# A decoder layer on one core: smaller DMA scratch, probability buffers of two heads, and other places for the feed-forward's tiles

## The chip, the cores and the metric

The kernel is one program on one core of a Trainium2 chip. The metric is the device time of one execution in microseconds (us), lower is better. A core has five engines that run side by side, each through its own list of instructions in a fixed order: TensorE (PE, with weight loads shown as PEld), VectorE (DVE), ScalarE (ACT), GpSimd (POOL) and SyncE (SP, which here only starts DMAs). They meet through semaphores. SBUF is the on-chip memory with 128 partitions, PSUM holds matmul results.

## The reference, in short

One decoder layer over 1024 tokens of width 1024, in float32:

```
h = x + RMSNorm_post(Mixer(RMSNorm_pre(x)))
out = h + RMSNorm_post(SwiGLU(RMSNorm_pre(h)))

Mixer: proj = hn @ w_in; split into q, k/v of three branches, gates, u, v
  8 heads (2 groups of keys and values), each with three attention branches, biased by relative position:
    compressed blocks | selected blocks of 64 (top 16 of 16: all causal ones) | sliding window of 512
    o = gate0 * o_c + gate1 * o_s + gate2 * o_w        (a softmax in each branch)
  8 gMLP groups: gelu(u) * (causal w_s @ layer_norm(gelu(v)) + b_s)
  concat -> @ w_out
SwiGLU: (silu(h2 @ w_gate) * (h2 @ w_up)) @ w_down,  width 2816
```

## The kernel before

A float32 product is made of three matmuls: each operand is split into a high and a low part (`split`, line 167 on ACT for the high part, line 173 on DVE or POOL for the low one), and `mm3` (lines 183 to 185) adds hi x hi, hi x lo and lo x hi.

**Order of the work.** The program is written with a framework that puts every instruction in the order of its engine beforehand. `tc.high_priority(...)` moves a block ahead in that order (`HP`, `HP2` the logits, `HO` and `HF` the output projection and the norm behind it, `HQ` the loads of q, `HS` the normalization, `HV` the products with v); the framework also sets the semaphore waits, for data and for buffers that have to come free. Order and waits are fixed when the program is built.

1. *Projections and gMLP*, until about 248 us. The transposed inputs `xTh0`, `xTl0`, `xTh1`, `xTl1` are read by the last projections (`v_proj`).
2. *Attention*, from 248 to about 593 us: query tiles 7, 6, ..., 0 of 128 tokens; in a tile two groups with two head pairs each, 32 pairs in all (pairs 0 to 3 are tile 7, 16 to 19 tile 3, 20 to 23 tile 2, 28 to 31 tile 0). For a head PE computes logits into PSUM (banks `ps_a`, two of them), DVE adds the bias and takes the extremes while writing them into a buffer `L` (lines 655 and 659), ACT applies exp in place (698). For the pair POOL normalizes in place (709), PE transposes (722), ACT and DVE split (`ph`, `pl`), PE multiplies with `vt` and `vch` (729), and the result is split into `mixh` and `mixl`. `load_q` loads `qr` for the pair after next through SP and lets POOL split it into `qt`. In the second pair of the next tile `output_proj` is placed (its inputs `gmh` are loaded by POOL's queue, `xt` by SP's), in the last pair `pre_ffn`, which writes the normed rows `h2s` to `h2_scr` in DRAM.
3. *Feed-forward*. The tokens are halves 0 and 1, the inner dimension is halves too. `raw1` (half 1, name `b_r1t` in the trace) is loaded from `h2_scr` in four DMAs (779), `plain_raw` (the first weights) in four (790). Eight weight operands (four in `plain_op`, four in the ring `op`) and `b12`, `b22` are split from them, and `plain_pass(1)` makes the first 256 hidden columns for half 1 with 96 matmuls; `plain_pass(0)` does the same for half 0 with `raw0`, `b11`, `b21`. All other hidden columns are made by Strassen-Winograd pairs (`prep_pair`, `run_pair`), 20 units of seven products, with `t1` to `t4` made from `raw0` and `raw1`. They end at about 1034 us.
4. *Down projection* until 1249 us, with the hidden values reloaded from DRAM (`hidr`).

**Memory.** SBUF of a partition is given out from two ends: a left stack above the scratch of dynamic DMAs (16,384 bytes before), and a right stack down from the top. A pool that is opened later on the place of a closed one makes its first writers wait for the last users of each tile that lay there. The left stack in attention is, from below: constants, the rings `whi` and `wlo`, `pt`, `mix`, `late` (`gpost`, `xt`, `h1`, `gmh`, `h2s`), six `L` buffers of 6,912 bytes, `o` (`otmp`, `os`), `q` (`qr`, `qt`). On the right lie `kt0`, `kt1`, `vch`, `vt` and the bias tables `B`, `C`, `MW`. The six buffers `L0` to `L5` (L0 the lowest) are given to the heads in turn from the top, L5, L4, ..., L0, then L5 again. The seven feed-forward tiles of 16 KB each (`r1t4`, `b22`, `b12t3`, `t1`, `t2`, `b11`, `b21`) are opened on the right after attention; `plain_raw` uses the place of `b11`, `plain_op` that of `t1`, `b12` that of `b12t3`. Worked out from the sizes, before: `r1t4` lies where `kt0`, `kt1` and `vch` lay, `b22` on `vt`, `b12t3` on `vt` and the bias tables, `t1` on L5, `o` and `q`, `b11` on L0 to L2, `b21` on `late` and L0.

## Time and profile before

| what | value |
|---|---|
| time, median of 3 runs | 1255.89 us (1254.95 to 1257.32) |
| profiled execution | 1254.52 us, span from first to last instruction 1252.8 us |
| mean granted clock of TensorE | 0.987 of full speed |
| PE busy | 1212.1 us (97%), 6074 instructions |
| PEld busy | 1011.5 us (81%) |
| DVE busy | 918.8 us (73%) |
| ACT busy | 566.0 us (45%) |
| POOL busy | 400.8 us (32%) |

The span is that of the profiled execution, which took 1.4 us less than the median of the runs. Busy shares are means over stages with different limits. A clock of 0.50 is 1.2 GHz, 1.00 is 2.4 GHz. In a timeline a row gives start, duration, engine, line of the code, operation, written and read tiles, and in brackets the idle time of the engine before it with what ended it; xN means N instructions in a row that were put together.

### The profile page before, as it was taken

What the parts mean: (1) busy time and instruction counts of PE and PEld (TensorE: products, weight loads), DVE (VectorE), ACT (ScalarE), POOL (GpSimd) and SP (SyncE); (2) the same over time, 40 slices, a digit from 0 to 9 for tenths busy, and PEclk for the clock granted to TensorE, in tenths of its full rate; (3) what the DMA queues carried; (4) which work ended last, traced back from release to release, by engine and by line L of the source; (5) the groups of instructions that cost most, each with busy time, mean ns of one, the idle gap of its engine ahead of it and who ended that gap; (6) DMA issues with size and microseconds to landing.
All of it is one profiled execution on the core that took longest, in us unless ns stands there. A gap on an engine that the chain in (4) does not pass through costs nothing. (4 is left out here: it accounts for less than half of the span.)

```text
span 1252.8 us, 18246 instructions
## 1 busy us (share of the span) xinstructions
PE 1212.1 (97%) x6074; PEld 1011.5 (81%) x6074; DVE 918.8 (73%) x2064; ACT 566.0 (45%) x1260; POOL 400.8 (32%) x467
## 2 busy tenths in 40 slices
PE   6999999989999999999999999999999999999996
PEld 5888878968888888887777888888888888888885
DVE  5646247479788899876689877877787647588996
ACT  3423022157677778875644332333332324544541
POOL 2415112178445455642151222201221201132433
PEclk9999999979999999999899999999999999999999
DMA  7313452142221221213714333223233189333335
GB/s 251 88 66 86 134 187 78 57 133 60 66 58 43 65 64 62 75 56 106 272 40 140 107 118 127 93 88 109 90 126 126 55 284 363 113 110 85 101 120 191
DMA packets 106229, 143.86 MB, mean 115 GB/s; under 512 B 8120, under 2 KB 64792, under 8 KB 106136
## 3 DMA queue, kind: packets, MB, share of 16 engines
q1 hardware_dynamic: 99408, 132.90, 32.7%
q10 hardware_dynamic: 4424, 5.61, 1.3%
q0 software_dynamic: 2304, 4.20, 1.2%
q8 instruction: 48, 0.79, 0.3%
q14 instruction: 45, 0.37, 0.1%
HBM read 103.60 MB, written 40.71 MB: 115 GB/s over the span
## 5 line engine op out<-in xcount | busy, mean ns | idle before, releaser
L937 DVE TENSOR_TENSOR cc<-fb,cc 128x512 f32<-128x512 f32 x140 | 94.3, 686 | 59.4 <-PE fb L185 58.5
L709 POOL TENSOR_SCALAR L<-L,wts 128x64 f32<-128x64 f32 (+8 forms) x192 | 107.6, 584 | 83.7 <-DVE wts L704 50.2
L698 ACT ACTIVATE L<-L,mm 128x64 f32<-128x64 f32 (+8 forms) x192 | 116.2, 607 | 30.6 <-DVE mm L655 29.9
L826 POOL TENSOR_TENSOR cc<-sil 128x512 f32<-128x512 f32 x22 | 34.9, 1587 | 289.0 <-issue 227.2
L173 DVE TENSOR_TENSOR pl<-ps_t,ph 128x512 fp32r<-128x512 f32 (+2 forms) x168 | 102.8, 618 | 13.5 <-ACT ph L167 12.7
L167 ACT CAST ph<-ps_t 128x512 fp32r<-128x512 f32 (+2 forms) x168 | 87.4, 532 | 43.5 <-PE ps_t L722 37.5
L167 ACT CAST op<-s 128x512 fp32r<-128x512 f32 x80 | 49.4, 621 | 122.2 <-PE fb L185 109.3
L184 PE MATMUL fb<-wdo,hido 128*128 128x512 f32 x264 | 102.7, 389 | 0.0
L183 PE MATMUL fb<-wdo,hido 128*128 128x512 f32 x264 | 101.9, 389 | 0.0
L185 PE MATMUL fb<-wdo,hido 128*128 128x512 f32 x264 | 100.4, 389 | 0.0
L184 PE MATMUL fb<-b_b,op 128*128 128x512 f32 x256 | 99.6, 389 | 0.0
L185 PE MATMUL fb<-b_b,op 128*128 128x512 f32 x256 | 99.4, 389 | 0.0
L183 PE MATMUL fb<-b_b,op 128*128 128x512 f32 x256 | 99.3, 389 | 0.0
L722 PE MATMUL ps_t<-ident,L 128*128 128x128 f32 (+1 forms) x592 | 94.9, 278 | 1.1 <-DVE mm L655 0.5
L650 PE MATMUL ps_a<-kt,qt 128*128 128x448 f32 (+4 forms) x208 | 78.0, 379 | 7.1 <-DVE L L659 4.3
L173 DVE TENSOR_TENSOR hido<-hidr,hido 128x512 fp32r<-128x512 f32 x77 | 60.6, 799 | 27.2 <-ACT hido L167 27.0
L1016 POOL TENSOR_TENSOR tt<-wdr 128x512 f32<-128x512 f32 x22 | 36.0, 1642 | 134.7 <-DVE wdo L173 80.0
L722 PEld LDWEIGHTS ps_t<-ident,L 128*128 128x128 f32 (+1 forms) x592 | 69.4, 139 | 9.9 <-POOL L L709 1.4
L167 ACT CAST hido<-hidr 128x512 fp32r<-128x512 f32 x77 | 47.3, 619 | 66.3 <-PE fb L185 23.2
L167 ACT CAST op<-wraw 128x512 fp32r<-128x512 f32 x60 | 37.0, 622 | 87.3 <-PE fb L185 71.3
L173 DVE TENSOR_TENSOR op<-s,op 128x512 fp32r<-128x512 f32 x80 | 63.3, 796 | 16.3 <-ACT op L167 15.6
L729 PE MATMUL ps_p<-ph,vt 128*128 128x256 f32 x264 | 73.2, 295 | 0.2 <-ACT ph L167 0.2
(351 smaller groups left out, 3480.0 us busy)
## 6 DMA issues: line engine op xcount, KB each, us to landing
wraw<-in_w_gate_up_dram SPq DMA_DIRECT2D x40, 512.0 KB, 3.6
hidr<-hid_scr SPq DMA_DIRECT2D x77, 256.0 KB, 2.7
hid_scr<-sil SPq DMA_DIRECT2D x44, 256.0 KB, 2.0
wdr<-in_w_down_dram SPq DMA_DIRECT2D x44, 256.0 KB, 5.3
hid_scr<-cc SPq DMA_DIRECT2D x33, 256.0 KB, 2.1
xt<-in_x_dram SPq DMA_DIRECT2D x16, 512.0 KB, 4.2
raw<-in_w_in_dram SPq DMA_DIRECT2D x16, 512.0 KB, 3.6
gm_scr<-gmt SPq DMA_DIRECT2D x16, 256.0 KB, 2.3
```

Source lines behind the costliest of these rows:

```text
L167: nc.scalar.copy(hi, src)
L173: e.tensor_tensor(lo, src, fl(hi), op=ALU.subtract)
L183: nc.tensor.matmul(ps, sh, mh, start=first, stop=False)
L184: nc.tensor.matmul(ps, sh, ml, start=False, stop=False)
L185: nc.tensor.matmul(ps, sl, mh, start=False, stop=last)
L650: nc.tensor.matmul(ps[:, :w], qt[:, 0, hh, :], kt_[g][:, c0:c0 + w], start=True, stop=False)
L698: nc.scalar.activation(L[:, c0:c1], L[:, c0:c1], AF.Exp, bias=mm[:, col:col + 1], scale=-1.0, accum_out=sums[:, hh, br:br + 1])
L709: nc.gpsimd.tensor_scalar(pts[hh][:, c0:c1], pts[hh][:, c0:c1], wts[:, hh, br:br + 1], 1.0, op0=ALU.mult, op1=ALU.mult)
L722: nc.tensor.transpose(ps[:kk, (bi * 2 + hh) * P:(bi * 2 + hh + 1) * P], pts[hh][:, c0:c0 + kk], ident)
L729: nc.tensor.matmul(pv[:, :256], v, ph[:kk, bi * 256:(bi + 1) * 256], start=(gi == 0 and bi == 0), stop=False)
L937: nc.vector.tensor_tensor(dst, ps, y_, op=ALU.add)
L1016: eng.tensor_tensor(dst, x_, y_, op=op)
```

## The change

The change has five parts.

- The program is built with a scratch for dynamic DMAs of 2,048 bytes (16,384 before), so the whole left stack lies 14,336 bytes lower.
- In attention `o` and `q` are opened below the `L` buffers and not above them.
- The `L` buffers are given out by hand. Tiles 7 to 4: in turn L5, L4, ..., L0, as before. Tile 3: index 4 - n % 5 with n the number of the head, that is L2, L1, L0, L4, L3, L2, L1, L0 for its eight heads. Tiles 2 to 0: one tile `[P, 2, 832]` for both heads of a pair, in L0, L2, L1, L0, ... by the number of the pair (pair 20, the first of tile 2, has L0).
- The feed-forward tiles are opened in another order: `b12t3`, `b22`, `t1`, `r1t4`, `b11`, `t2`, `b21`. Worked out from the sizes, after: `b12t3` lies on `kt0`, `kt1` and `vch`, `b22` on `vt`, `t1` on the bias tables and the beginning of `vt`, `r1t4` on the last 2,048 bytes of L5 and on free space above it, `b11` on L3 to L5, `t2` on L0 to L3, `b21` on `q` and L0. `q` itself lies where `xTh1` and `xTl1` lay.
- Loads and splits of the feed-forward's start stand in another order. Before: all of `raw1`, all of `plain_raw`, all eight operands, then `b12`, `b22`. After: `raw1` and the gate weights by halves in turn, then the up weights; the two halves of the first gate operand with `b12` and `b22` behind them in turn, the first up operand, then the operands of the second 128 columns.

No matmul, split, reduction or transfer is added or removed. The diff:

```diff
@@ -524,10 +524,9 @@
 
     g_at = []
     at = {}
-    for nm in ("pt", "mix", "late", "L", "o", "q"):
+    for nm in ("pt", "mix", "late", "o", "q", "L"):
         if nm == "L":
             at[nm] = Ring("at_L", 6, "left")
-            at[nm].pools.reverse()
             g_at.append(at[nm])
             continue
         g_, at[nm] = pool("at_" + nm, 1, "left")
@@ -613,6 +612,17 @@
                                     gffn[:, 4 * b:4 * b + 4, None].to_broadcast([P, 4, P]), op=ALU.mult)
             nc.sync.dma_start(out=h2_scr[i // 4][:, 4 * b:4 * b + 4, (i % 4) * P:(i % 4 + 1) * P], in_=tl)
 
+    lturn = {"n": 0}
+
+    def lring(i):
+        n = lturn["n"]
+        lturn["n"] += 1
+        ps_ = at["L"].pools
+        return ps_[5 - n % 6][1] if i > 3 else ps_[4 - n % 5][1]
+
+    def lpair(n):
+        return at["L"].pools[2 - n % 3][1]
+
     for ti, i in enumerate(TILES):
         na = 64 + P * (i + 1)
         nw = P * min(i + 1, 5)
@@ -637,10 +647,12 @@
                 pts = []
                 sums = small.tile([P, 2, 3], F32, name="sums")
                 with tc.high_priority(HP if i >= 4 else HP2):
+                    if i <= 2:
+                        Lp = lpair(at_).tile([P, 2, 832], F32, name="L")
                     for hh in range(2):
                         r = pr * 2 + hh
                         h = g * R + r
-                        L = at["L"].tile([P, 64 + S + 640], F32, "L")
+                        L = Lp[:, hh] if i <= 2 else lring(i).tile([P, 64 + S + 640], F32, name="L")
                         pts.append(L)
                         mm = small.tile([P, 8], F32, name="mm", bufs=6)
 
@@ -757,7 +769,7 @@
     PF_T1, PF_T2, PF_T3, PF_T4 = 2, 2, 2, 2
     g_b = []
     bps = {}
-    for tag in ("r1t4", "b22", "b12t3", "t1", "t2", "b11", "b21"):
+    for tag in ("b12t3", "b22", "t1", "r1t4", "b11", "t2", "b21"):
         g_, bps[tag] = pool("ffn_" + tag, 1, "right")
         g_b.append(g_)
 
@@ -772,14 +784,13 @@
     def bsplit(dst, src, k, pool_from=HK):
         split(dst[:, 0, k], dst[:, 1, k], src, "act", "dve" if k < pool_from else "pool")
 
-    def h2_load(dst, half):
-        for a in range(2):
+    def h2_load(dst, half, *parts):
+        for a in parts or range(2):
             for kq in range(2):
                 k = a * HK + 2 * kq
                 nc.sync.dma_start(out=dst[:, a, 2 * kq:2 * kq + 2], in_=h2_scr[half][:, k:k + 2, :])
 
     raw1 = btile("r1t4", F32)
-    h2_load(raw1, 1)
     b12 = btile("b12t3")
     b22 = btile("b22")
 
@@ -837,16 +848,24 @@
     praw = bps["b11"].tile([P, 2, 2, HK, 256], F32, name="plain_raw", tag="b11")
     pop = bps["t1"].tile([P, 4, 2, HK, P], F32R, name="plain_op", tag="t1")
     plain = {}
+    def plain_op(m, j, a):
+        plain.setdefault((m, j), [None, None])[a] = operand(praw[:, m, a, :, j * P:(j + 1) * P],
+                                                            pop[:, 2 * m + a] if j == 0 else None)
+
+    for a in range(2):
+        h2_load(raw1, 1, a)
+        load_w(praw[:, 0, a], 0, 0, a)
+    for a in range(2):
+        load_w(praw[:, 1, a], 1, 0, a)
+    for a, dst in enumerate((b12, b22)):
+        plain_op(0, 0, a)
+        for k in range(HK):
+            bsplit(dst, raw1[:, a, k], k)
+    for a in range(2):
+        plain_op(1, 0, a)
     for m in range(2):
         for a in range(2):
-            load_w(praw[:, m, a], m, 0, a)
-    for j in range(2):
-        for m in range(2):
-            plain[m, j] = [operand(praw[:, m, a, :, j * P:(j + 1) * P], pop[:, 2 * m + a] if j == 0 else None)
-                           for a in range(2)]
-    for a, dst in enumerate((b12, b22)):
-        for k in range(HK):
-            bsplit(dst, raw1[:, a, k], k)
+            plain_op(m, 1, a)
 
     def plain_pass(half, blo, bhi):
         for j in range(2):
@@ -1162,7 +1181,7 @@
     import concourse.tile as _tile
     from concourse.bass_utils import run_bass_kernel_spmd as _run
 
-    nc = _bacc.Bacc("TRN2", target_bir_lowering=False, num_devices=1)
+    nc = _bacc.Bacc("TRN2", target_bir_lowering=False, num_devices=1, dynamic_dma_scratch_size=2048)
     arrays, args = {}, []
     feeds = [(n, np.ascontiguousarray(inputs[n])) for n in _INS] + list(shape_constants().items())
     for name, a in feeds:
```

## Rows read from the trace of the kernel before

**Rows 1.** Windows: length, busy PE, PEld, DVE, ACT, POOL; clock, DMA share, GB/s.

```profile
500.00:525.00 25.00, 24.54 (x156) 21.11 (x154) 22.88 (x112) 22.35 (x71) 13.02 (x27) 1.00 0.17 54
...
575.00:600.00 25.00, 21.21 (x99) 16.11 (x98) 13.62 (x39) 13.53 (x37) 5.56 (x15) 0.93 0.44 152
600.00:625.00 25.00, 24.87 (x106) 19.86 (x105) 15.59 (x27) 14.98 (x27) 3.37 (x2) 0.93 0.68 236
...
650.00:675.00 25.00, 21.74 (x84) 16.16 (x83) 20.05 (x26) 10.19 (x18) 9.32 (x7) 0.93 0.37 116
675.00:700.00 25.00, 25.00 (x112) 20.67 (x112) 24.95 (x38) 10.55 (x19) 5.09 (x4) 1.00 0.39 126
```

**Rows 2.** Windows at the start of the feed-forward, same columns.

```profile
594.00:598.00 4.00, 2.93 (x6) 1.82 (x6) 1.56 (x5) 1.62 (x4) 0.00 (x0) 0.58 1.08 398
598.00:600.00 2.00, 0.36 (x2) 0.30 (x2) 1.29 (x4) 2.00 (x7) 0.46 (x1) 0.99 1.02 416
600.00:602.00 2.00, 2.00 (x8) 1.36 (x7) 2.00 (x4) 2.00 (x6) 0.09 (x1) 0.86 1.02 392
602.00:604.00 2.00, 2.00 (x6) 1.51 (x6) 2.00 (x5) 2.00 (x5) 0.00 (x0) 0.50 1.09 383
604.00:606.00 2.00, 2.00 (x9) 1.59 (x8) 2.00 (x5) 2.00 (x4) 0.00 (x0) 0.79 1.09 383
```

**Rows 3.** Timeline of SP's DMA queue, 588 to 600: start, us, line, operation.

```profile
592.01 2.10 SPq L779 DMA_DIRECT2D b_r1t<-h_scr  x4
594.15 3.85 SPq L790 DMA_DIRECT2D plain_raw<-in_w_gate_up_dram  x3
```

**Rows 4.** Timeline of PE, 593 to 600; in brackets idle time before.

```profile
594.99 0.79 PE L183 MATMUL ps_w<-whi,mixh 128*128 128x512 f32 x1 [1.46 <-ACT mixh L167]
...
599.64 0.50 PE L183 MATMUL ps_a<-b_b12t,plain_op 128*128 128x512 f32 x1 [1.73 <-ACT b_b12t L167]
```

**Rows 5.** Timelines of ACT, DVE and POOL, 597 to 625.

```profile
597.81 0.60 ACT L590 ACTIVATE h<-ps_w 128x512 f32<-128x512 f32 x1
...
623.96 2.33 ACT L167 CAST b_b<-raw 128x512 fp32r<-128x512 f32 x4 [7.09 <-DMA raw<-h_scr]
...
597.91 0.68 DVE L173 TENSOR_TENSOR plain_op<-plain_raw,plain_op 128x512 fp32r<-128x512 f32 x1
...
599.54 0.55 POOL L179 TENSOR_TENSOR rstd<-ms,mhalf 128x1 f32<-128x1 f32 x1 [13.56 <-DVE ms L177]
608.46 3.27 POOL L179 TENSOR_TENSOR rstd<-ms,mhalf 128x1 f32<-128x1 f32 x1 [8.37 <-DVE ms L177]
```

**Rows 6.** PE's waits, 654 to 668: waiter <- releaser: us, times, longest.

```profile
PE fb L185 <- DVE op L173: 1.6, 2, 1.3
```

**Rows 7.** Timelines of DVE, POOL and PE around pairs 19 and 20.

```profile
492.31 0.22 DVE L655 CUSTOM_DVE_ANT_0 L<-ps_a,C 128x64 f32<-128x64 f32 x1
...
494.43 3.29 POOL L709 TENSOR_SCALAR L<-L,wts 128x64 f32<-128x64 f32 x6 [2.75 <-DVE wts L704]
...
502.15 2.86 POOL L709 TENSOR_SCALAR L<-L,wts 128x64 f32<-128x64 f32 x6 [3.21 <-ACT ph L167]
...
502.81 1.04 PE L722 MATMUL ps_t<-ident,L 128*128 128x128 f32 x8
```

**Rows 8.** Timelines of PE and POOL at the start of attention.

```profile
240.89 0.29 PE L185 MATMUL ps_t<-whi,xTl 128*128 128x280 f32 x1
...
248.06 0.54 PE L650 MATMUL ps_a<-kt,qt 128*128 128x448 f32 x2
...
243.43 1.42 POOL L173 TENSOR_TENSOR qt<-qr,qt 128x256 fp32r<-128x256 f32 x2
```

**Rows 9.** DMA issues of the kernel: KB each, median us to landing.

```profile
qr<-q_scr SPq DMA_DIRECT2D x64, 64.0 KB, 2.4
...
gmh<-gm_scr POOLq DMA_DIRECT2D x16, 256.0 KB, 3.1
...
plain_raw<-in_w_gate_up_dram SPq DMA_DIRECT2D x4, 512.0 KB, 8.8
```

## The prediction

> **What bounds the kernel now.** I read the busy shares first: PE is busy 1212.1 of 1252.8 us, so the whole idle time of the kernel on PE is 40.7 us, and an edit can only pay where PE idles or runs at its lower clock. Then PE in stretches of 25 us [rows 1]: from 675 us on it is full, at 25.00 us for 112 matmuls, 0.223 us each. In 575:600 it idles 3.79 us, in 600:625 0.13 us, in 650:675 3.26 us, and in each of the three the granted clock averages 0.93, which costs another 0.07 x 25 = 1.75 us. Together 7.18 + 5.25 = 12.4 us: the ceiling for what the change can give back, since these are the stretches that its tiles and loads touch.
>
> The fine windows [rows 2] show the first of them: from 598 to 600 PE is busy 0.36 of 2 us, and from 600 to 606 the clock is 0.86, 0.50, 0.79, that is at 1.2 of 2.4 GHz for part of it, just after PE had stood still; 2 x (0.14 + 0.50 + 0.21) = 1.7 us lost. The DMA queue [rows 3] says why: the feed-forward inputs (`raw1`) and first weights (`plain_raw`) are issued from 592.0 to 598.0 us, seven of the eight in these two rows and one `plain_raw` half a microsecond ahead. On PE itself [rows 4] the last six matmuls of the output projection start at 594.99 after a wait of 1.46 us for the last `mixh`, and the first matmul of the plain pass waits 1.73 us more for `b_b12t`, which is split behind weights that had just landed.
>
> What comes after is the other half. `plain_pass(0)` needs `raw0`, which needs the norm of the last query tile. That chain [rows 5] leaves the projection at 597.81 and has its first `raw0` split at 623.96: 26.2 us. PE begins `plain_pass(0)` then with almost no wait (0.13 us idle in 600:625), because `plain_pass(1)` lasted until then. Behind it the t-tiles and the first pair's operands keep PE waiting at 654 to 664 on DVE [rows 6]; all of that work starts from `raw0`.
>
> **The change part by part.** It adds and removes no matmul, split, reduction or DMA: the same 96 matmuls, 16 + 16 split halves and eight 512 KB loads stand in another order over other addresses. So every term is a wait.
>
> *Scratch and order of tags.* The left stack starts 14,336 bytes lower. `r1t4` (`raw1`) now touches only the end of L5, `b11` (`plain_raw`) L3 to L5. L5 is last used by tile 4, L4 and L3 by the second and third pair of tile 3. So both loads can be issued in tile 3 or soon after it, once the last `h2s` of tile 4 is stored, and not at 592; tile 3's last pair is transposed from 502.81 on [rows 7], so that is some 505 us or a little later. Removed on the path: the 1.73 us wait [rows 4], and the 1.7 us of low clock that followed it [rows 2]. The 1.46 us wait stays: it is the chain of the last PV product. The splits still have to be made: `plain_op` lies on `vt` and waits for the last PV product at 593.5, `b12` for `vch` at about 592. From 594 to 598 DVE is busy 1.56 of 4 us and ACT 1.62 [rows 2], and a split half takes 0.58 us on ACT and 0.68 us on DVE [rows 5], so some 8 of the 16 can be done before PE asks. From then on one split feeds three matmuls, 0.68 us against 3 x 0.223 = 0.67 us, so PE is just fed. Without that cover PE would wait 0.6 us for each late split, at most 8 x 0.6 = 4.8 us, which gives back the gain. I take 1.73 + 1.7 = 3.4 us.
>
> *What is late next.* With PE 3.4 us ahead, `raw0` must come 3.4 us earlier too, or PE stands at `plain_pass(0)`. Of the chain's 26.2 us several are queueing behind splits: the second rstd on POOL takes 3.27 us where the first takes 0.55 [rows 5], with DVE streaming splits beside it; that alone is 2.7 us. With half the splits done before 598, I take 5 us off the chain (bounds: 0, if the remaining splits fall into it again, and 9). Then PE is not held, and the DVE work behind [rows 6] begins 5.0 - 3.4 = 1.6 us earlier against PE, which takes 1.6 us off the 3.26 + 1.75 us in 650:675. Gain so far 3.4 + 1.6 = 5.0 us.
>
> *Tiles 2 to 0 with pair buffers.* Three buffers for two heads hold what six held for one: nothing. Tile 3 has five buffers instead of six: by the trace each buffer that its eight heads are now given was free before that head's first write. But pair 20, the first of tile 2, is given L0, which the second head of pair 19 has just filled. Pair 20's first write is at 492.31; pair 19's transposes end at 503.85 [rows 7]. Nothing writes L0 in between now. Queued behind it on DVE are only pair 20's own writes and those of pairs 21 to 23; on PE, pair 20's logits hold both `ps_a` banks, so pair 21 waits too, and for pair 20 the normalization on POOL and the transposes. POOL has normalized pair 19 by 497.72, so with nothing else in front PE could finish its transposes near 499.5 and pair 20 starts 7 us late. From its first write to its normalized values took 505.01 - 492.31 = 12.7 us in a full queue; DVE has been idle meanwhile and may do it in 11, so the values are there at about 510.5 and not at 505.01. PE has pair 19's PV products and part of the projection to fill that with. Bounds: 0, if that fills it, and 7 us, if nothing does. PE idles 0.46 us in this stretch now and DVE has 2.1 us free [rows 1], so later pairs catch up slowly; I take 1.0 us, near the lower end, because after 525 us the pairs wait for PE and not for DVE.
>
> *Start of attention.* `q` now lies over `xTh1` and `xTl1`, so its loads go out after PE's last read of them at about 241.2 and not before it. A `qr` load lands in 2.4 us [rows 9]; the second step of POOL's splits takes 1.42 us for two pairs and ended at 244.85 [rows 8]. With 241.2 + 2.4 + about 2.2 for both steps, `qt` is there at 245.8. The first logits stand at 248.06 behind projection matmuls in PE's order, so up to 2.5 us are covered by these; if that cover were gone, 1.0 to 2.5 us. I take 0.6 us.
>
> *Loads moved.* Eight loads of 512 KB pass into attention, in front of `qr`, `xt` and `h2s` on SP's queue. In the old place four landed in 8.8 us [rows 9]. `qr` is loaded two pairs ahead, and two pairs take some 14 us of POOL's order (one follows the other by 502.15 - 494.43 = 7.7 us [rows 7]), so such a delay is covered; uncovered it would cost 8.8 - 2.4 = 6.4 us of one pair's wait, most of it filled by the pairs between. I take 0. The Trainium skill ("DMA: Bandwidth & Descriptors", Issuing engines are not separate DMA queues) says that DMAs of all issuing engines run on the same 16 engines and interleave; by that rule the small loads are late as well, and with those 6.4 us uncovered at one pair the sum would be a loss of 3 us. The trace agrees so far as the 16 engines were full, at shares of 1.02 to 1.09, while those loads and the first pair's ran [rows 2].
>
> *Scratch itself.* Only `gmh` is issued by POOL, two loads a tile; 16 in all, 3.1 us to landing [rows 9]. If 2 KB could not hold two of them, POOL would wait up to 3.1 us in each of eight tiles, with `qt` splits and normalizations queued behind; I take 0, since the four pairs of a tile lie between two such loads. The same page (SWDGE vs HWDGE vs iDMA) says that the rings lie in that carveout, at 16 bytes a descriptor; by it 2 KB is 128 entries an engine, an estimate, far above two loads, and no run here shows it.
>
> *End of the feed-forward's first half.* Three of the four `hidr` buffers lie on `b21`, where two did, and the fourth is free, so the first load comes no later. I take 0; if it came late, PE would wait for one landing, some 3.1 us by `gmh` of the same size [rows 9].
>
> Sum: 5.0 - 1.0 - 0.6 = 3.4 us off the profiled execution's 1254.52 us, 1251.1. That execution is 1.4 us under the median of the runs, 1255.89, so I state 1252.5.
>
> **The rivals.** *Pair 20 decides (slower).* The hole is not filled: 6 us at 500 to 515, 1.5 us at the start, and a chain gain of only 3 us: 1255.9 + 4.5 = 1260.4. For it: PE and DVE are both above 90% there. Against it: PE's backlog after 525. It decides from 5 us of PE idle between 495 and 530. *The gain stops at `raw0`.* The norm chain is no faster, PE only waits later, at 620 to 624; gain 0 to 1.6, costs 1.6: 1255.9 to 1257. For it: the chain is 26.2 us long against 96 x 0.223 = 21.4 us of plain pass. This is also what would be seen if SP's order issued the loads late, as before. *The whole stall goes.* The chain shortens by 9 us, DVE is ready before PE, and 650:675 fills up: 5.1 + 4.5 - 1.6 = 8 us, 1247.9. *POOL or SP held by the moved loads*: 3 us or more at one tile, 1259.
>
> **How the numbers follow.** 0.2% is 2.5 us, about what this kernel's runs can tell from no change. Forecast (1249.5 to 1255.0) 0.42, of which 0.06 lies within 0.2%; the whole stall goes 0.13; stopped at `raw0` 0.22, of which 0.06 slower; pair 20 decides 0.18; loads 0.05. Faster 0.36 + 0.13 = 0.49, same 0.06 + 0.16 = 0.22, slower 0.06 + 0.18 + 0.05 = 0.29. The range takes in both the stall that goes and the pair that waits, 1247.5 to 1260.0; what lies outside is the worse half of the slower cases and a little below.
>
> **What would show it.** Right: SP issues `b_r1t` and `plain_raw` before 530; the first plain matmul follows the projection without a wait; no low clock in the 6 us behind; the first `raw0` split comes 4 to 6 us earlier after the last PV product; 650:675 loses 1 to 2 us less. Wrong: DVE's writes into L pause by more than 8 us before tile 2 and PE idles over 3 us there; or PE waits for `b_b` at the head of `plain_pass(0)`; or PE waits at the first logits after the projections end.

## The result and the profile after

The kernel became slower. After: 1273.09 us median of 4 runs (1272.24 to 1276.3); before, run beside it: 1256.61 (1254.95 to 1258.29). Ratio 1.0128, 95% interval 1.0099 to 1.0157. The forecast was 1252.5, with a range of 1247.5 to 1260: it missed by 20 us, on the wrong side. The profiled execution took 1273.58 us, its span is 1271.9 (before 1252.8). PE is busy 1214.3 us (before 1212.1), with the same 6074 matmuls, so of the 19.1 us some two, net, are matmuls at the lower clock; everything else is waits.

To see where they arise I read six moments from the timelines and compared them:

| moment, us | before | after | added in the stretch |
|---|---|---|---|
| first logits | 248.1 | 248.0 | -0.1 |
| normalization of pair 16 (POOL, first row) | 467.53 | 472.26 | +4.8 |
| end of the last PV product | 593.5 | 600.9 | +2.7 |
| last matmul of the feed-forward's first half | 1033.8 | 1043.4 | +2.2 |
| end of the down projection | 1213.3 | 1232.4 | +9.5 |
| span | 1252.8 | 1271.9 | 0 |

The stretches are cut from one timeline, so they add up by construction, and each is read from one execution. How far a single reading carries: in the five kernels of runs 1, 5 and 6 below, whose edits lie behind pair 16, its normalization came 4.0, 5.2, 3.8, 4.6 and 14.1 us later than in the kernel before.

So the largest loss lies where the prediction had put nothing, 430 us behind the edited order. Windows of the kernel after, columns as in [rows 1]:

```profile
275.00:300.00 25.00, 21.32 (x135) 18.31 (x132) 22.87 (x71) 15.50 (x39) 21.63 (x24) 0.93 0.31 95
500.00:525.00 25.00, 23.62 (x134) 19.12 (x134) 21.79 (x92) 19.29 (x57) 10.37 (x20) 1.00 0.72 238
575.00:600.00 25.00, 23.67 (x132) 18.58 (x130) 18.23 (x65) 18.02 (x55) 5.19 (x14) 1.00 0.24 68
600.00:625.00 25.00, 22.56 (x93) 18.34 (x93) 13.94 (x27) 15.51 (x30) 1.10 (x2) 0.93 0.36 121
625.00:650.00 25.00, 17.68 (x72) 14.29 (x71) 16.00 (x27) 7.76 (x15) 1.16 (x1) 0.80 0.35 116
650.00:675.00 25.00, 23.74 (x105) 19.33 (x104) 20.62 (x20) 10.55 (x19) 20.77 (x12) 1.00 0.19 65
...
1025.00:1050.00 25.00, 21.32 (x91) 16.72 (x89) 12.69 (x15) 5.80 (x11) 7.61 (x6) 0.96 0.82 278
1050.00:1075.00 25.00, 23.12 (x91) 18.56 (x92) 15.87 (x24) 10.29 (x18) 1.57 (x1) 0.90 0.87 314
```

The same windows of the kernel before, where [rows 1] doesn't show them:

```profile
275.00:300.00 25.00, 23.78 (x154) 19.66 (x153) 22.95 (x81) 17.59 (x42) 23.33 (x25) 1.00 0.31 91
1025.00:1050.00 25.00, 25.00 (x112) 20.67 (x111) 22.76 (x30) 10.59 (x18) 8.75 (x6) 1.00 0.88 307
1050.00:1075.00 25.00, 25.00 (x112) 20.71 (x111) 12.65 (x20) 11.12 (x20) 0.00 (x0) 1.00 0.83 313
```

Before, PE was full from 1025 to 1075; after, it idles 3.68 + 1.88 us there and runs at 0.96 and 0.90, another 1.0 + 2.5 us: 9.1 of the 9.5 us. In 275:300 PE loses 2.46 us more to idling than before and 1.75 to the clock, in 500:525 0.92 us more to idling. Around the start of the feed-forward the windows have to be read with care, for they stand at fixed times and attention now ends 7.4 us later: 575:600 has 2.5 us less idle time than in [rows 1] because it holds nothing behind attention now, and the waits of the join have moved into 600:625, which idles 2.3 us more. 650:675 has 2.0 us less idle time and the full clock, as hoped; but 625:650, full before, idles 7.32 us at a clock of 0.80.

**Down projection.** ACT and PE around the join, timelines as in [rows 4]:

```profile
1043.48 2.70 ACT L167 CAST wdo<-wdr 128x512 fp32r<-128x512 f32 x5 [12.98 <-PE fb L185]
1046.09 0.62 ACT L167 CAST hido<-hidr 128x512 fp32r<-128x512 f32 x1
...
1046.76 0.50 PE L183 MATMUL fb<-wdo,hido 128*128 128x512 f32 x1 [3.32 <-ACT hido L167]
...
1054.58 1.94 PE L185 MATMUL fb<-wdo,hido 128*128 128x512 f32 x4 [1.88 <-DVE hido L173]
```

ACT stood 12.98 us at a split into `wdo`, the weight operands of the down projection, until PE's last matmul of the first half, at 1043.44, and the `hido` splits stood behind it in ACT's queue. Worked out from the sizes, the second `wdo` buffer begins on the place that the tag `r1t4` has now. The code puts `t4` into that tag, and `t4` is read by the last of the seven products of a unit. Before, `t1` lay there, which is read fourth.

**Start of the feed-forward.** SP's queue, PE, ACT and DVE after, against [rows 3 to 5]:

```profile
498.96 2.03 SPq L801 DMA_DIRECT2D plain_raw<-in_w_gate_up_dram  x4
...
510.20 2.75 SPq L791 DMA_DIRECT2D b_r1t<-h_scr  x4
```

```profile
599.81 0.38 PE L743 MATMUL ps_p<-pl,vch 64*128 64x256 f32 x1
...
603.38 0.50 PE L183 MATMUL ps_a<-b_b12t,plain_op 128*128 128x512 f32 x1 [2.44 <-ACT plain_op L167]
...
613.28 0.39 PE L183 MATMUL ps_w<-whi,mixh 128*128 128x512 f32 x1
...
615.10 0.61 PE L185 MATMUL ps_w<-whi,mixl 128*128 128x512 f32 x2
```

```profile
600.23 2.18 ACT L167 CAST b_b12t<-b_r1t 128x512 fp32r<-128x512 f32 x4 [0.69 <-PE ps_p L743]
...
606.87 0.30 ACT L167 CAST mixh<-os 128x128 fp32r<-128x128 f32 x1
...
635.93 1.14 ACT L167 CAST b_b<-raw 128x512 fp32r<-128x512 f32 x2 [10.67 <-DMA raw<-h_scr]
...
600.88 2.50 DVE L173 TENSOR_TENSOR b_b12t<-b_r1t,b_b12t 128x512 fp32r<-128x512 f32 x4 [0.62 <-ACT b_b12t L167]
603.30 0.57 DVE L748 TENSOR_TENSOR os<-ps_p,otmp 64x128 f32<-64x128 f32 x2
```

The loads do go out 82 to 93 us earlier. But `b12` now lies on `kt0`, `kt1` and `vch`, and ACT's first split into it, at 600.23, waits for the last product with `vch`, which ends at 600.19; no split of it was made ahead. PE's first plain matmul still waits, 2.44 us. Then the order in which the program was built shows: four splits of `b12`, two of `plain_op`, four of `b22`, two more stand on ACT ahead of the last `mixh`, `os` on DVE behind four low halves, and on PE the last part of the output projection stands behind the first plain matmuls. It begins at 613.28 and ends 14.8 us after the last PV product; before it was 4.4 us. Before, two things held the plain matmuls behind the projection: `plain_op` lay on `o` among others, where `os` is, and the weights landed only after the last `mixh`, as ACT's rows of the kernel before show:

```profile
594.64 0.30 ACT L167 CAST mixh<-os 128x128 fp32r<-128x128 f32 x1 [0.65 <-DVE os L736]
596.65 0.62 ACT L167 CAST op<-plain_raw 128x512 fp32r<-128x512 f32 x1 [1.72 <-DMA plain_raw<-in_w_gate_up_dram]
```

Which of the two kept the order no run separates. The chain from the end of the projection to `raw0` is indeed shorter, 20.2 us against 26.1 [rows 5], but it starts 10.4 us later, and PE, with its plain matmuls already spent, waits for `b_b`, by PE's waits from 600 to 680 (waiter, releaser: us in total, times, longest):

```profile
PE fb L183 <- ACT b_b L167: 7.3, 1, 7.3
```

**Start of attention.** SP's queue after, and then before:

```profile
240.61 1.32 SPq L544 DMA_DIRECT2D qr<-q_scr  x2
241.97 0.59 SPq L509 DMA_DIRECT2D B<-s_scr  x1
242.61 15.21 SPq L544 DMA_DIRECT2D qr<-q_scr  x10
257.86 1.07 SPq L130 DMA_DIRECT2D wo_raw<-in_w_out_dram  x2
```

```profile
231.22 0.37 SPq L509 DMA_DIRECT2D B<-s_scr  x1
231.63 19.59 SPq L545 DMA_DIRECT2D qr<-q_scr  x12
252.94 0.83 SPq L130 DMA_DIRECT2D wo_raw<-in_w_out_dram  x2
```

The first `qr` goes out 9 us later, as predicted, and the first logits are not later, nearly as predicted. What the prediction left out is what stands behind those loads on SP's queue: the first weights of the output projection, `wo_raw`, 4.92 us later. POOL splits them in front of the first normalizations and stands still for them; its first split of them before, and then DVE and POOL after:

```profile
259.54 1.04 POOL L161 TENSOR_SCALAR whi<-wo_raw 128x1024 fp32r<-128x1024 f32 x1
```

```profile
276.06 3.80 DVE L713 TENSOR_SCALAR wts<-sums 128x6 f32<-128x6 f32 x1
...
263.20 1.05 POOL L161 TENSOR_SCALAR whi<-wo_raw 128x1024 fp32r<-128x1024 f32 x1 [3.42 <-DMA wo_raw<-in_w_out_dram]
...
275.73 2.41 POOL L162 TENSOR_TENSOR wlo<-wo_raw,whi 128x1024 fp32r<-128x1024 f32 x1
278.06 0.75 POOL L173 TENSOR_TENSOR qt<-qr,qt 128x256 fp32r<-128x256 f32 x1
278.75 1.07 POOL L161 TENSOR_SCALAR whi<-wo_raw 128x1024 fp32r<-128x1024 f32 x1
282.29 2.81 POOL L721 TENSOR_SCALAR L<-L,wts 128x64 f32<-128x64 f32 x4 [2.46 <-DVE wts L716]
```

The first normalization comes 3.5 us later (267.69 against 264.22). Behind it an operation on six elements a partition took 3.80 us on DVE and ended at 279.86, when POOL's unbroken row of splits ended at 279.82. In the kernel before, the 32 operations of this line took 0.17 us in the median and 1.05 at most. From here on the normalizations of pairs 1 to 16 are about 4.75 us late, 1.3 us more than the first.

**Pair 20.** The end of pair 19's transposes on PE, DVE's next write into an `L` buffer, and pair 20's normalization on POOL, the last against 502.15 before [rows 7]:

```profile
505.88 0.66 PE L734 MATMUL ps_t<-ident,L 128*128 128x128 f32 x4 [0.16 <-DVE pl L173]
...
506.95 0.21 DVE L667 CUSTOM_DVE_ANT_0 L<-ps_a,C 128x64 f32<-128x64 f32 x1
...
514.90 2.86 POOL L721 TENSOR_SCALAR L<-L,wts 128x64 f32<-128x64 f32 x6 [2.73 <-DVE wts L716]
```

It comes 12.75 us later, of which 4.19 are the lag that pair 19 has too. DVE had written nothing into these buffers for 10.0 us, since 496.97.

### The profile page after: what moved, and what is told of

The parts are those of the page before. It is cut to its first block, busy times and chain, and to the rows that moved or that the text cites. A ratio compares the mean times of both kernels' runs of the same rounds, so it can differ in the third digit from the quotient of the medians.

```text
span 1271.9 us, 18213 instructions
## 1 busy us (share of the span) xinstructions
PE 1214.3 (95%) x6074; PEld 1013.0 (80%) x6074; DVE 923.5 (73%) x2064; ACT 566.3 (45%) x1260; POOL 401.7 (32%) x467
## 5 line engine op out<-in xcount | busy, mean ns | idle before, releaser
L183 PE MATMUL fb<-wdo,hido 128*128 128x512 f32 x264 | 103.5, 395 | 3.7 <-ACT hido L167 3.7
L184 PE MATMUL fb<-wdo,hido 128*128 128x512 f32 x264 | 103.9, 394 | 0.0
L185 PE MATMUL fb<-wdo,hido 128*128 128x512 f32 x264 | 102.1, 393 | 1.9 <-DVE hido L173 1.9
L662 PE MATMUL ps_a<-kt,qt 128*128 128x448 f32 (+4 forms) x208 | 78.1, 378 | 10.8 <-DVE L L671 7.8
```

Of the source, the lines that this page charges most:

```text
L183: nc.tensor.matmul(ps, sh, mh, start=first, stop=False)
L184: nc.tensor.matmul(ps, sh, ml, start=False, stop=False)
L185: nc.tensor.matmul(ps, sl, mh, start=False, stop=last)
L662: nc.tensor.matmul(ps[:, :w], qt[:, 0, hh, :], kt_[g][:, c0:c0 + w], start=True, stop=False)
```

## The experiments

All kernels but three are the kernel after with edits; those three start from the kernel before, and the text says so. Medians are of 4 runs where no number is given; ratios are against the kernel before on the same occasion, whose median moved between 1256.1 and 1257.0 us from one occasion to another.

**1. `t4` and `t1` exchanged.** `t1` into the tag `r1t4`, `t4` into `t1`:

```diff
-    t1 = btile("t1")
-    for k in range(HK):
-        bsplit(t1, raw0[:, 0, k], k, PF_T1)
...
-    t4_ = btile("r1t4")
+    t1 = btile("r1t4")
+    for k in range(HK):
+        bsplit(t1, raw0[:, 0, k], k, PF_T1)
+    t4_ = btile("t1")
```

> The changed kernel, in which t4 and t1 have changed places: t4, which the last of the seven products of a pair reads, lies in the tile t1 (bias tables and vt), and t1, read by the fourth product, in r1t4. Theory: of the 19.1 us that the changed kernel's profile is longer than the one before (1271.9 against 1252.8 us of span), 9.5 come at the change to the down projection, because the second wdo buffer lies on r1t4, so ScalarE's queue stands there until the last product has read t4 (12.98 us idle before the wdo casts at 1043.48), and the hido casts stand behind it. Then the wait of 3.32 us before the first down matmul, the 1.88 us behind it and the low clock go: some 8 to 9 us, 1264 to 1265.5. Rival: the down projection is late because hidr lies over b21 and because SP's queue puts it behind the wdr loads; then nothing changes, 1273. A cost of up to 2 us is possible at the first pair, because t1 is now the last of the four to be split.

Measured: 1265.69 us (1264.16 to 1265.95), ratio 1.0077 [1.0059, 1.0094]: 7.4 us less than the kernel after. Its windows at the join:

```profile
1025.00:1050.00 25.00, 25.00 (x112) 20.62 (x111) 14.63 (x22) 7.61 (x13) 3.87 (x3) 1.00 0.85 290
1050.00:1075.00 25.00, 25.00 (x110) 20.36 (x110) 16.83 (x21) 10.55 (x19) 5.27 (x4) 1.00 0.92 331
```

PE is full again at full clock. The cause of the largest term is shown: which of seven products reads last the tile under `wdo`. From the end of the first half to that of the down projection the profile now has 179.9 us (179.5 before, 189.0 in the kernel after). The seven other kernels of runs 2 to 6 that leave `t4` where it is have 187.3 in this stretch, so the place costs 7.8 us, and the 9.5 of the table is the high reading of one execution. From the last PV product to the end of the first half it took 444.6 us, where the kernel after has 442.5; the expectation allowed for that, but no run shows its reason.

**2. The first `qr` loads issued by ACT**, so that nothing on SP's queue stands behind their wait:

```diff
-    def load_q(i, g, pr):
+    def load_q(i, g, pr, eng=nc.sync):
...
-            nc.sync.dma_start(out=qr[64 * dup:64 * dup + 64],
+            eng.dma_start(out=qr[64 * dup:64 * dup + 64],
...
-        qts[key] = load_q(*key)
+        qts[key] = load_q(*key, nc.scalar)
```

> The changed kernel, with the first two pairs' qr loads issued by ScalarE's queue instead of SP's, so that the load of the bias table B is first on SP again. Theory: attention starts 4.75 us later than before because B stands on SP's queue behind the first qr, which waits for xTh1 and xTl1 since q was moved over them (B issued at 241.97 and not at 231.22); C, the first bias writes and the next qr wait for it. With B at 231 the offset of the normalizations falls from 4.75 to under 1 us, and the whole to about 1268.5. Rival: qr itself comes too late at its new place; then the offset stays at 3 to 4.75 us and the time at 1272 to 1273.

Measured: 1274.86 us (1271.64 to 1276.42), ratio 1.0149 [1.0127, 1.0171]: no gain. `B` did go out at 231.66 and the first logits at 245.4, but `wo_raw` still at 256.86, behind eight `qr` loads that start at 245.68. The normalization of pair 16 was still 3.8 us late. So `B` was not the point; the passage of six pairs' `qr` through two buffers is left, and run 3 tries it.

**3. The tag `q` off `xTh1` and `xTl1`**, by opening it between `L` buffers 2 and 3 (in `load_q`, `qt` is also taken ahead of `qr`):

```diff
-    for nm in ("pt", "mix", "late", "o", "q", "L"):
-        if nm == "L":
-            at[nm] = Ring("at_L", 6, "left")
+    for nm in ("pt", "mix", "late", "o", "L", "q", "M"):
+        if nm in "LM":
+            at[nm] = Ring("at_" + nm, 3, "left")
...
+    at["L"].pools += at["M"].pools
```

> The changed kernel, with q opened between the third and the fourth L buffer (and qt ahead of qr in it), so that qr no longer lies where xTh1 and xTl1 lay; every other place of the change stays. Theory, after the run with the first q loads on ScalarE's queue (B on time at 231.66, offset still 3.8 us): what sets the offset is the load of wo_raw, which stands on SP's queue behind six pairs of q loads that pass through two qr buffers; that chain begins at 240.61 and not at 231.63, wo_raw goes out at 257.86 and not at 252.94, GpSimd's split of it ends late, and the first normalization stands behind it. In the three kernels so far wo_raw's delay (4.92 and 3.92 us) and the offset (4.75 and 3.83 us) go together. With q off xTh1 the first qr goes out near 231, wo_raw at 253 to 254, the offset is under 1 us and the time near 1268.5. Rival: the offset comes from the order of the first logits on PE, and stays at 3 to 4.75: 1272 to 1273.

Measured: 1272.48 us (1269.27 to 1276.35), ratio 1.0121 [1.0087, 1.0156]: no gain that the runs can tell. In its profile, of an execution of 1269.27 us, `wo_raw` went out at 253.78, and pair 0 was 1.0 us late in place of 3.5; but from pair 1 on the lag was 2.2 us, and between the two `wts<-sums` again took long, 3.04 us at 274.31. So SP's queue makes some 2.5 us of the term, by the profile; 1.3 us come in beside the small operation, here as in the kernel after; and 1.0 us is left, with `wo_raw` still 0.84 us late.

**4. The small operation on ACT.** The guard against a sum of zero as an addition on ACT:

```diff
-                nc.vector.tensor_scalar(wts, sums, 1e-30, None, op0=ALU.max)
+                nc.scalar.activation(wts, sums, AF.Copy, bias=1e-30)
```

> The changed kernel, with the guard of the sums (wts<-sums, 128x6 elements, the maximum with 1e-30) taken from VectorE to ScalarE as sum + 1e-30. Theory: with q off xT, wo_raw went out 0.84 us after that of before and the first normalization came 0.99 us late, but the second was 2.25 us late: behind a VectorE operation of 6 elements a partition that took 3.80 us at 276.06 in the changed kernel (0.15 at its shortest, 0.60 at this place before), and ended at 279.86, when GpSimd's unbroken chain of splits ended (279.82). It waits for GpSimd. Without it on VectorE the second pair's offset falls to that of the first, 3.5 us, and the time by 1.3 us or somewhat more (all 32 of these operations take 10.7 us of VectorE, 7.7 before): 1270 to 1272. Rival: another VectorE operation takes its place and waits as long; offset 4.75, 1273.

Measured: 1266.38 us (1266.02 to 1268.83), ratio 1.0078 [1.0056, 1.01]: 6.7 us less, more than expected. In its profile the lag of the normalizations shrank from 3.0 us at pair 0 to 0.6 at pair 3, but it was 3.3 again at pair 16. Whether the 6.7 us are the wait was asked with the same edit in the kernel before, without and with the 2 KB scratch:

> The kernel before, with the guard of the softmax sums (wts<-sums) on ScalarE and nothing else. Theory (a small VectorE operation that starts under a chain of GpSimd work is held until that chain ends; it cost the kernel after at its start, where the guard took 3.80 us): in the kernel before the longest such guard took 1.05 us, so there is little to free, 0 to 2 us: 1254.5 to 1256.9 beside a before of 1256.9. Rival (the 6.7 us of the run with the guard on ScalarE came from ScalarE being the better place for it anywhere): some 5 us less here too, about 1251.

Measured: 1253.58 us (1251.86 to 1255.7, 11 runs), ratio 0.9973 [0.996, 0.9986]. The fastest kernel of the study, 2.9 us under the kernel before; a little more than the theory allowed, less than the rival. The normalizations of four kernels against those of the kernel before, us later:

| pair | 0 | 1 | 2 | 3 | 16 |
|---|---|---|---|---|---|
| after | 3.5 | 4.7 | 4.8 | 4.7 | 4.7 |
| run 3, `q` off `xTh1` and `xTl1` | 1.0 | 2.2 | 2.2 | 2.2 | 2.2 |
| run 4, guard on ACT | 3.0 | 2.0 | 1.1 | 0.6 | 3.3 |
| before, guard on ACT | -0.6 | -1.5 | -2.5 | -3.2 | -1.2 |

So the edit brings the first normalizations forward in the kernel before too. With the guard on ACT in both, the kernel after is 3.6 us behind at pair 0 and still at pair 1, where the lag otherwise grows from 3.5 to 4.7; and in run 2, where no guard took more than 1.04 us, it doesn't grow either (3.0 and 2.5). That the 1.3 us between these pairs are DVE's long operation fits both. But little of it lasts: at pair 16 the lag is 4.5 with the guard on ACT in both, and 3.8 in run 2. Of the 7.6 us that run 4's profile is shorter, 1.5 are there by pair 16, 3.5 come between it and the last PV product, 1.0 in the rest of the first half and 1.6 at the join.

> The kernel before with the 2 KB scratch and the guard on ScalarE. The scratch alone gave 1254.5. Theory: the guard adds nothing that can be measured, 1252.5 to 1255. Rival (ScalarE is the better place anywhere): 1249 to 1250.

Measured: 1262.54 us (1260.83 to 1263.97, 8 runs), ratio 1.0039 [1.0021, 1.0056]. Both expectations missed. Against the scratch alone (run 8) the same edit costs 8 us here. By the profiles 2.0 us of it are there at pair 16, 3.6 come between pair 16 and the last PV product, and 2.6 from there to the end of the first half. The loss begins at the start of attention: in 285:290 PE idles 1.28 us, and behind it the clock falls,

```profile
285.00:290.00 5.00, 3.72 (x20) 2.69 (x18) 4.53 (x17) 3.54 (x8) 4.85 (x5) 0.90 0.36 105
290.00:295.00 5.00, 5.00 (x33) 4.91 (x32) 3.10 (x12) 3.13 (x8) 3.16 (x5) 0.76 0.44 131
```

where the kernel with the scratch alone idles 0.02 and 0.43 us at 1.00. So ACT is not the better place for the guard as such: -6.7, -2.9 and +8.0 us with the same line. That DVE's operation took 3.80 us in the kernel after is shown; what a move of it is worth depends on where the work around it then falls, and I can't predict that from these runs.

**5. Pair 20 on the buffers that were read longest ago** (L2 and not L0):

```diff
-        return at["L"].pools[2 - n % 3][1]
+        return at["L"].pools[2 - (n + 1) % 3][1]
```

> The changed kernel, with the three pair buffers given out one step further: pair 20 has L2, pair 21 L1, pair 22 L0. Theory: pair 20 waited for L0, filled just before by pair 19 (its normalization came 12.75 us after that of before, where the offset had been 4.75), and that cost 2.7 us of the time from the first to the last product with v. On L2, which pair 18 leaves two pairs earlier, the normalization of pair 20 comes within 6 us of the one before, and 2 to 3 us go: 1270.5. Rival: tiles 2 to 0 lose by having three pair buffers instead of six single ones; then pairs 21 to 23 stay 12 us late and the time stays at 1273.

Measured: 1269.73 us (1267.18 to 1279.91), ratio 1.0126 [1.0082, 1.0171]; one run of the four lies far off, so the median says little, the profile more. Pair 20's normalization:

```profile
508.53 2.89 POOL L721 TENSOR_SCALAR L<-L,wts 128x64 f32<-128x64 f32 x6 [2.62 <-DVE mm L667]
```

6.4 us later than before, where pair 19 was 4.7 late, so 1.7 of its own in place of 8.6. The lag at the last PV product is 6.0 and at pair 16 5.2, so about 0.8 is added behind the start in place of 2.7. Six other kernels that leave pair 20 on L0 (runs 1, 2, 3 and 6) add 2.4 to 2.7 there: the term is real, some 2 us. Run 4, with the guard on ACT, is the exception, with 0.8 us less than before in this stretch.

**6. The last output projection ahead of the splits.** One element of `b12`, `b22` and `plain_op` is written from the last `mixl`, so their first splits have to wait for it:

```diff
+    wout_last = wout_args[TILES[-1]][1]
...
+    for t_ in (b12, b22, pop):
+        nc.vector.tensor_copy(t_[0:1, 0, 0, 0, 0:1] if t_ is pop else t_[0:1, 0, 0, 0:1], wout_last[0:1, 3, 0:1])
```

> The changed kernel with three copies of one element from the last mixl into b12, b22 and plain_op, ahead of their splits: the split of each first slice, and so the plain pass, then comes behind the last head pair's result, as before the change, where plain_op lay on o and q. Three tiny VectorE operations are added, nothing else changes. Theory: the 7.32 us of waiting at the head of the pass over half 0 and the low clock behind it come from the order: with the operands ready early, the last output projection was put behind 36 matmuls of the plain pass, and mixh behind twelve splits on ScalarE, so that the projection left PE 14.6 us after the last product with v, and not 4.3 us as before. With the projection first raw0's first split comes 25 to 28 us after the last product with v (35.0 in the changed kernel, 30.4 before) and 5 to 9 us go: 1264 to 1268. Rival: the chain from the projection to raw0 is as long as the plain pass whatever the order, and PE waits elsewhere: 1272 to 1274.

Measured: 1268.24 us (1266.36 to 1269.27), ratio 1.0102 [1.0082, 1.0122]: 4.9 us less. PE's wait at `plain_pass(0)` is gone; there is one at the projection in its place:

```profile
604.67 0.80 PE L183 MATMUL ps_w<-whi,mixh 128*128 128x512 f32 x1 [4.70 <-ACT mixh L167]
```

That wait is 4.70 us where the kernel before has 1.46 [rows 4], since the remaining early splits still stand on ACT and DVE. Two further orders tried to get rid of it:

```diff
+    nc.vector.tensor_copy(b22[0:1, 0, :, 0], wout_last[0:1, 3, 0:4])
+    nc.vector.tensor_copy(pop[0:1, :, 0, :, 0], wout_last[0:1, 3, 0:16].rearrange("p (a b) -> p a b", b=4))
```

> The changed kernel, with all splits into b22 and plain_op behind the last mixl (two copies of a few elements added on VectorE), those into b12 free to come early. Theory: in the run with the projection first, the last mixh still stood behind nine splits on ScalarE; here it stands behind the four of b12 alone, and PE has twelve matmuls of the plain pass that need only b12 to fill that time. The projection leaves PE within 6 us of the last product with v (7.6 with the projection first, 14.7 in the changed kernel), raw0's first split comes 25 to 28 us after it, and the time is 2 to 4 us under that run: 1264 to 1266. Rival: the splits of b22 and plain_op, now later, hold PE in the plain pass by as much; then it is 1268 again.

Measured: 1274.84 us (1271.18 to 1277.85), ratio 1.0138 [1.0104, 1.0171]. A miss: PE waits 3.1 us for `os` and 3.7 us at `plain_pass(0)`. The second one puts `b12` behind the tail as well (`for t_ in (b12, b22)` with the first of these lines):

> The changed kernel, with every split into b12, b22 and plain_op behind the last mixl (three small copies added on VectorE). Theory: in the two kernels that held back a part of these splits the last head pair's tail was still late, since os stood behind the low halves of b12 on VectorE (PE waited 3.1 us for it) or mixh behind nine splits on ScalarE. With none in front the projection leaves PE 4 to 5 us after the last product with v (4.4 before, 7.6 and 9.0 in those two, 14.8 in the changed kernel), raw0's first split comes some 26 to 28 us after it (30.4 before), and the stretch from there to the end of the feed-forward takes 434 to 437 us (442.5 in the changed kernel, 440.3 before, 437.9 with the projection first): 1264 to 1268. Rival: the plain pass, now with splits that feed it late, takes longer by what the chain wins: 438 to 441 us, 1269 to 1272.

Measured: 1275.53 us (1271.35 to 1280.41), ratio 1.0146 [1.0114, 1.0178]. A miss too. In the profiled execution, of 1280.41 us, pair 16 was 14.1 us late, 9.4 more than in the kernel after: time was lost at the start of attention again. DVE and POOL there:

```profile
290.22 6.54 DVE L173 TENSOR_TENSOR mixl<-os,mixh 128x128 fp32r<-128x128 f32 x1
...
294.89 0.71 POOL L173 TENSOR_TENSOR qt<-qr,qt 128x256 fp32r<-128x256 f32 x1
295.58 1.03 POOL L161 TENSOR_SCALAR whi<-wo_raw 128x1024 fp32r<-128x1024 f32 x1
```

Another small DVE operation took 6.54 us and ended at 296.76, POOL's unbroken row at 296.61. Two of the four times lie near 1271.6, so this loss may not be in all of them. But the order brought nothing either: the projection left PE 3.1 us after the last PV product, sooner than expected, yet PE waited 6.4 us for `b_b` at `plain_pass(0)`, and from the last PV product to the end of the first half it took 441.6 us (442.5 in the kernel after, 437.9 with the first order). The rival had said 438 to 441 for it.

**7. Repairs together.** The edits of 1, 3 and 5 and the second order of 6:

> The changed kernel with four edits together: t4 and t1 changed, q between the L buffers, pair 20 on L2, and the last mixh ahead of the splits of b22 and plain_op. If the four causes are independent, their gains add: 7.4 measured, some 4.7, 2 to 3 and 7 to 8 us, together 21 to 23 off 1273.1, so 1250 to 1252, below the kernel before. If they share a stall (a later stage waits for the same thing whoever is early), the sum comes out at 1254 to 1258.

Measured: 1256.31 us (1254.27 to 1258.83, 12 runs), ratio 0.9988 [0.9969, 1.0007]: level with the kernel before. With the guard on ACT as well, and the third order of run 6 in place of the second:

> The changed kernel with t4 and t1 changed, q between the L buffers, pair 20 on L2, every split of the feed-forward's start behind the last mixl, and the guard of the sums on ScalarE. The run with four edits came to 1256.3, level with the kernel before. Theory: the guard brings 1 to 2 us and the tail in front another 1 to 3: 1252 to 1254.5, below the kernel before (1256.9). If VectorE's wait moves to another operation and the plain pass gives the rest back, 1256 again.

Measured: 1259.64 us (1256.54 to 1265.03, 12 runs), ratio 1.0021 [1.0005, 1.0038], a miss: with the tail first the chain from the projection to `raw0` took 27.0 us again, as before (26.1), and PE waited 4.7 us for `b_b`. Last, the edits of 1, 3 and 5 and the guard on ACT, with the first order of 6 and then without any:

> The kernel after with t4 and t1 exchanged, the tag of q off xTh1 and xTl1, pair 20 on the group that was read longest ago, the last output projection ahead of the splits, and the guard on ScalarE. If the early loads of the feed-forward bring something once the rest of the change's costs are gone (theory: the 3.4 us of the prediction, or a part of them, are there): 1251 to 1254. Rival (the splits must stand either ahead of the last projection or in the chain to raw0, so that the early loads bring nothing whatever else is mended): 1255 to 1258, level with the kernel before.

Measured: 1255.89 us (1254.78 to 1257.89, 12 runs), ratio 0.9987 [0.9972, 1.0002].

> As the run beside it, without the edit that puts the last output projection ahead. Theory: the projection behind 36 plain matmuls costs what the exchange of that order alone gave, about 4 us: 1255 to 1260. Rival (only the chain to raw0 counts, and it is the same 26 us either way): the same as the run beside it within 1 us.

Measured: 1260.76 us (1259.57 to 1265.19, 12 runs), ratio 1.0033 [1.0019, 1.0048]. Between these two the projection put ahead is worth 4.9 us, as alone. The first, in which PE still waits 4.7 us for the last `mixh`, has 438.8 us from the last PV product to the end of the first half, the kernel before 440.3, and the kernel before with the small scratch, whose loads are late, 437.0. The early loads bring nothing that stands out of that.

**8. The scratch alone**, in the kernel before:

```diff
-    nc = _bacc.Bacc("TRN2", target_bir_lowering=False, num_devices=1)
+    nc = _bacc.Bacc("TRN2", target_bir_lowering=False, num_devices=1, dynamic_dma_scratch_size=2048)
```

> The kernel before with the scratch of 2 KB and nothing else: the left stack 14,336 bytes lower, all tags and orders as before. Theory: the scratch itself costs nothing (two gmh loads a tile are all that GpSimd issues), and no last-read tile of the feed-forward falls under the down projection's first buffers: 1254 to 1258, no change. Rival: GpSimd waits for room for its descriptors, or the shift alone costs at a boundary: 3 us or more.

Measured: 1254.5 us (1253.36 to 1255.31, 10 runs), ratio 0.9976 [0.996, 0.9993]. In the time 2 KB of scratch costs nothing. The profile is not that of the kernel before, though: the first logits come 12.5 us earlier, `wo_raw` goes out 2.7 us later, the last PV product ends 2.8 us later, and the stretch from there to the end of the first half is 3.3 us shorter. The shift of the left stack moves waits about, and here they cancel.

## Why the prediction was wrong

**"End of the feed-forward's first half", taken at 0, is the largest loss, 9.5 us.** The step looked at `hidr`, whose place was indeed free, and not at what else is opened there: `wdo`. No stretch in [rows 1 to 8] lies behind 700 us. A table of each new tile with the tile below it and that tile's last reader was made for the start of the feed-forward, and it had to be made for its end too. Run 1 shows the cause; it gives back 7.4 us in the median, and 7.8 is what seven other profiles show for the place.

**The gain at the feed-forward's start, 3.4 + 1.6, did not come; the stretch lost 2.2.** That the loads go out around 505 was right (498.96 and 510.20), and so was that `b12` waits for `vch`, and that some 8 splits can be done before PE asks: of `b12` and `plain_op` alone five high and four low halves were done at 603.38. The step that failed is the one behind it: "PE is just fed" priced the splits against PE only, and not against the tail of attention, which needs ACT and DVE too. `otmp`, `os` and `mixh` stood behind these splits, and the projection on PE stood behind 36 plain matmuls. Nor did the 1.73 us wait go; it is 2.44. Whether the old address of `plain_op` or the late weights had kept the order before is open. The 5 us taken off the chain to `raw0` were about right (5.9, of which 2.7 are the second rstd as the prediction said: 0.55 us at 623.53 in place of 3.27), but it began 10.4 us later. Run 6 shows the order's part, 4.9 us twice. The 2.2 us are the whole stretch to the end of the first half, in which the lost and the won add up. The rival that the gain stops at `raw0` had the place right, and not that the norm itself could move behind it.

**Start of attention, taken at 0.6, measured 4.8.** The first logits were priced, and were not late. The step named the moved loads and not what stands behind them on SP's queue, `wo_raw`, nor who waits for that: POOL, and with it every normalization. That is 3.5 us at pair 0, of which run 3 takes 2.5 away, in the profile and not clear of noise in the time. Another 1.3 us come in between pairs 0 and 1, beside DVE's long operation, which no row of the prediction had; runs 2 and 4 agree with that cause, and leave open how much of it reaches pair 16.

**Pair 20, taken at 1.0, measured 2.7.** The mechanism was right, the size was not: its values come 8.6 us late by its own lag in place of 5.5. What was mis-sized is the moment at which L0 comes free: the prediction let PE end pair 19's transposes 1.8 us after its normalization (499.5 against 497.72), and it took 4.6 us (506.54 against 501.97), since PE had other products in front. From the first write to the normalized values it took 10.8 us, where 11 were forecast. More than a quarter of the lag reaches the end, where less than a fifth was taken. Run 5 takes some 2 us of it away.

**Scratch at 0, moved loads at 0**: right by run 8 for the scratch, in the time; for the loads nothing in the profile speaks against it, and no run separates them.

With all four places mended the time is that of the kernel before (1255.89 us, ratio 0.9987, in run 7), so the forecast gain is not there either. What stays open: how far the early loads could bring something in an order that neither holds back the tail nor `raw0` (four orders gave one stall or the other), where the 6.7 us of run 4 come from, and why the guard on ACT gains in two kernels and loses 8 us in a third.

## What to carry to other kernels

When tiles change places, list for every tile of every later phase, also those hundreds of microseconds on, what lies below it and which instruction reads that last; between two tiles of equal size, the one read last goes where no early writer follows. An address or a late load that seems only a delay may be what keeps a critical tail ahead of fill-in work, so look at what can pass it before removing it. For a moved DMA follow the queue to the next transfers of another kind behind it, and price those.

## What was not expected of the hardware

A VectorE operation on 128 x 6 elements, 0.17 us in the median, took 3.80 us in the kernel after and 3.04 us in run 3, and one on 128 x 128 (two SBUF inputs) 6.54 us in the order with the tail first; in all three its end lies within 0.2 us of the end of a row of GpSimd instructions without a gap (in the first, 279.86 and 279.82). A larger DVE operation that reads PSUM, `pl<-ps_t,ph` just before the first of them, took its usual 0.69 us beside the same row. The Trainium skill ("GPSIMD Engine Reference", Specifications) says that GpSimd's SBUF interfaces are shared with VectorE and contend with operations in a two-port mode or with two SBUF inputs. The traces agree for the operation on 128 x 128; whether the one on six elements, with one input, is of the other kind no run here shows.

The Trainium skill also says ("SBUF — State Buffer", SBUF: two separate sides) that whichever starts first holds the pair for its whole instruction. By that the wait would end with the GpSimd instruction that was running, in the first case at 278.14. Most waits here do: in the kernel before, 52 DVE operations that began under a GpSimd instruction took over 0.9 us longer than the median of their kind (the same line and tiles), and 50 of them ended within 0.6 us of the end of that instruction, also where GpSimd went on without a gap, as here to 289.75 (DVE, then POOL):

```profile
282.68 1.71 DVE L173 TENSOR_TENSOR mixl<-os,mixh 128x128 fp32r<-128x128 f32 x1
...
281.88 2.37 POOL L162 TENSOR_TENSOR wlo<-wo_raw,whi 128x1024 fp32r<-128x1024 f32 x1
284.22 1.08 POOL L161 TENSOR_SCALAR whi<-wo_raw 128x1024 fp32r<-128x1024 f32 x1
```

The three long ones didn't: the 3.80 and the 3.04 us lasted through two further GpSimd instructions, the 6.54 us through five. So a DVE operation that waits can be passed by the next GpSimd instruction; what decides it no run shows.

At the join of the kernel after, the granted clock fell after each of PE's two waits: behind 3.32 us at 1046.76 and 1.88 us at 1054.58 it was 0.96 and 0.90 in the two windows, so 5.2 us of waiting cost 9.
